# Single 4 KB places for the rows and weights of the first stage, and a first half of x loaded ahead from two queues

## The chip, the cores and the metric

The kernel runs on one core of a Trainium2 chip. The metric is the device time of one execution in microseconds (us). Comparisons use runs of both kernels on the same chip.

## What is computed

One residual block over 1024 tokens of width 1024: three token mixers (a gated linear recurrence, a forgetting attention, and a cross-attention into 256 memory tokens) with sigmoid merge gates, an output projection, and a convolutional gated feed-forward. The first stage of the kernel holds the beginning of it:

```python
h = _rmsnorm(x, norm_mix_g[l])
z = h @ w_in[l]
(hq, hf, hi, hg, fq, fk, fv, ff, mq, gate_logits) = split(z, pts)
...
mem_kv = _rmsnorm(mem, norm_mem_g[l]) @ mem_kv_w[l]
y_c = _memory_mixer(mq, mem_kv, mem_q_norm_g[l], mem_k_norm_g[l])
gates = sigmoid(gate_logits).reshape(B, T, N_BRANCH, D_MODEL)
merged = (gates[:, :, 0] * (y_a @ w_br_hgrn[l]) + gates[:, :, 1] * (y_b @ w_br_fox[l])
          + gates[:, :, 2] * (y_c @ w_br_mem[l]))
x = x + merged @ w_out[l]
x = x + _conv_glu_ffn(_rmsnorm(x, norm_ffn_g[l]), ...)
```

The row norm of x is a factor per token. The kernel multiplies by the gain of the norm first, runs the matmuls on x times gain, and applies the factor (`rt`, spread to `rx`) to the result.

## The kernel before

Every operand of a matmul is split into a high part (`wh`, `uh`), cast on ACT, and a low part (`wl`, `ul`), subtracted on DVE; `mm3` makes three matmuls of each product: high by high, high by low, low by high. A product of 128 x 128 weights with 512 columns is one such group of three.

The first stage is a list of steps, `SEQ`, which the kernel issues one after the other. A scheduler of the framework then places the instructions of each engine by its own estimate of when they can run; each engine takes its instructions in the order so built. The steps that matter here:

- `w0` to `w4` (`first_weights`) split the weights of the first two gate chunks, which lie in `wg[0]` and `wg[1]`. `x0` to `x7` (`x_chunk`) make `uh` and `ul` from the row blocks `xk` of x. `s0` to `s7` (`gate_step`) run the 12 matmuls of one k for two gate chunks and two column halves, 96 in all, into PSUM tiles `lg`, `tr` and `po`.
- `u0` to `u7` (`mem_chunk`) split the memory tokens `mt`; `mn` squares the rows of the memory for their norm.
- `k0` to `k7` (`kv_chunk`) split one quarter of the memory's key or value weights each (`wkv`, 128 x 1024) and run 12 matmuls; k0 to k3 give the keys, k4 to k7 the values. `me` (`keys_out`) normalizes the keys, `mv` writes the values out, `mk` transposes the keys.
- `xn` (`x_norm`) squares the eight row tiles of x, `x_row`, on ACT and DVE in turns, and makes `rt`.
- `f1`, `f2`, `f3` (`differences`) make the operand families T1, T2, T3 of the later dense units from `xk`; T1 and T2 reuse the memory of the row tiles.
- `c0` (`first_cover`) runs the third gate chunk, "the cover": 48 matmuls with the weights `cover_raw`, among which `spread_dma` (PE transpose, ACT copy, two DMAs) spreads `rt` to `rx`. `ev` evaluates the two first gate chunks with `rx`.

Ten matmuls on a constant tile (`NDULL`, line 263), the fillers, run on PE ahead of everything.

`wg`, the memory rows, `wkv` and `x_row` pass through four tiles of two rows each (8 KB of a partition): `T2h` and `T2l` hold `wg` and `wkv`, `T1h` and `T1l` the memory rows and the rows of x. All loads of the stage are issued by the sync engine SP in the order written:

```python
SP.dma_start(cv, vec)
for k in range(KC):
    if k in (0, 2):
        SP.dma_start(wg[k // 2], w_first[k // 2])
    SP.dma_start(xk[k], xT[:, k, :])
```

then the memory, its rows, four `wkv`, the constants, four rows of x, and from there one `wkv` and one row of x in turns. The first cover weights come last in the text. SP takes its queue in order too: a load whose place is still in use holds back those behind it.

After the stage come a fourth gate chunk, the dense units, the attention stages, and the feed-forward, which the change does not touch except for names of tiles.

Of the kernel before, what the change touches and what calls it, by code (L numbers as in the profile page):

```python
# [8 lines left out]
F32 = mybir.dt.float32  # L9
F32R = mybir.dt.float32r  # L10
# [4 lines left out]
P = 128  # L15
T = 1024
# [10 lines left out]

ORDER = [(br, j) for br in (1, 0, 2) for j in range(8)]
NCOVER, NPAIR = 2, 10
NDULL = 10  # L30
NFOX = [0, 3, 0, 3, 0, 3, 1]

_dense = [12, 13, 14, 15] + [16 + 8 * br + j for br, j in ORDER[4:4 + NPAIR]]
# [5 lines left out]
FOX_STEPS, HGRN_STEPS, MEM_STEPS = 28, 14, 7  # L39
AHEAD = 300  # L40
FOX_LATE = 0.2
SEQ = ("w0 x0 s0 w1 x1 s1 w2 x2 s2 w3 x3 s3 w4 x4 s4 x5 s5 x6 s6 x7 s7 u0 u1 u2 u3 mn u4 u5 u6 u7 k0 k1 k2 k3 me k4 k5 k6 k7 mv xn f1 c0 f2 ev mk f3").split()
WFIRST = {0: (0, 1), 1: (1, 2), 2: (2, 3), 3: (3, 4), 4: (4, 8)}
TMIN = -(1.0 - 2.0 ** -24)

# [63 lines left out]
def tile_block(ctx: ExitStack, tc: tile.TileContext, xT, memT, x_rows, mem_rows, vec, fbias, mats, hmask, w_first, w_cm, w_hi, w_fqk, w_fv,  # L109
# [63 lines left out]
    def rstd_small(out, ss, n):  # L173
        w = ss.shape[1]
        V.tensor_scalar(out, ss, 1.0 / n, EPS, ALU.mult, ALU.add)
        return G.tensor_tensor(out, out, mhalf[:, :w], ALU.pow)
# [60 lines left out]
    p0 = Rounded(tc, name="p0", bufs=1, side="right", reuse_waits="tile")  # L237
    fam = {}

    def new_family(pool, name):  # L240
        fam[name] = [pool.tile([P, 4, HB], F32R, tag=f"{name}{p}", name=f"{name}{p}") for p in "hl"]

    pairs = {}

    def row_tile(name):
        t, i, p = pairs.get(name, (None, 2, "l" if name == "T1" else "h"))
        if i == 2:
            p = "hl"[p == "h"] if t is not None else p
            t, i = pt.tile([P, 2, T], F32, tag=name + p, name=f"row{name}"), 0
        pairs[name] = (t, i + 1, p)  # L250
        return t[:, i, :]

    for name in ("T1h", "T1l", "T2h", "T2l"):
        pt.tile([P, 2, T], F32, tag=name, name=f"place{name}")
    umh, uml = (pt.tile([P, KC, NM], F32R, tag=f"T3{p}", name=f"um{p}") for p in "hl")
    mkf = p0.tile([P, 4, NM], F32, tag="mkf", name="mkf")
    mt = p0.tile([P, KC, NM], F32, tag="mt", name="mt")

# [3 lines left out]
    for _ in range(NDULL):  # L262
        PE.matmul(ps_tr()[:, :P], mhalf[:, 0:1].to_broadcast([P, P]), dull, start=True, stop=True)

    wg = [row_tile("T2") for i in range(2)]

    def load_wkv(q):
        wkv.append(row_tile("T2"))
        late["wkv"] = SP.dma_start(wkv[q], w_mkv[q])

    def load_row(i):
        nonlocal last_row
        x_row.append(row_tile("T1"))
        last_row = SP.dma_start(x_row[i], x_rows[i])

    wkv, mem_row, x_row, last_row = [], [], [], None
    SP.dma_start(cv, vec)
    for k in range(KC):
        if k in (0, 2):
            SP.dma_start(wg[k // 2], w_first[k // 2])  # L280
        SP.dma_start(xk[k], xT[:, k, :])
    SP.dma_start(mt, memT)
    for i in range(2):
        mem_row.append(row_tile("T1"))
        SP.dma_start(mem_row[i], mem_rows[i])
    for q in range(4):
        load_wkv(q)
    SP.dma_start(ones, mats[:, P:P + 1])
    SP.dma_start(ident, mats[:, 0:P])
    for i in range(4):  # L290
        load_row(i)
    for i in range(4):
        load_wkv(4 + i)
        load_row(4 + i)
    br, j = order[2]
    cover_raw = raw_weights(w_cm[16 + 8 * br + j], KC * P)
    warm = cp.tile([P, 1], F32, tag="warm", name="warm")
    S.activation(warm, mhalf[:, 0:1], AF.Exp)

# [125 lines left out]
    def gate_step(k):  # L425
        h, l = gw[k // 4]
        for n in range(2):
            for i in range(2):
                sl = slice(n * HB, (n + 1) * HB)
                ws = slice((k % 4) * 256 + i * P, (k % 4) * 256 + (i + 1) * P)  # L430
                mm3(gps[i][n], h[:, ws], l[:, ws], uh[k][:, sl], ul[k][:, sl], k == 0, k == KC - 1)

    def x_norm():
        for i in range(8):
            if i % 2:
                V.tensor_tensor_reduce(out=x_row[i], in0=x_row[i], in1=x_row[i], op0=ALU.mult, op1=ALU.add, scale=1.0,
                                       scalar=0.0, accum_out=rt[:, i:i + 1])
            else:
                late["square"] = S.activation(x_row[i], x_row[i], AF.Square, accum_out=rt[:, i:i + 1])
        rstd_small(rt, rt, D)  # L440

    ybd = tc.dram_tile([P, 4, T], F32, name="ybd")

# [24 lines left out]
    cover = gates_early(NCOVER - 1)  # L468

    def first_cover():  # L470
        wh, wl = weights(None, (KC, P), cover_raw)
        spread = ps_proj()
        pss = [ps_proj(), ps_proj()]
        for n, ps in enumerate(pss):
            sl = slice(n * HB, (n + 1) * HB)
            for k in range(KC):
                late["cover"] = mm3(ps, wh[:, k, :], wl[:, k, :], uh[k][:, sl], ul[k][:, sl], k == 0, k == KC - 1)
                if (n, k) == (0, 2):
                    with tc.issue_after(late["cover"].ins):
                        spread_dma(rx, rt, p0.tile([P, P], F32, tag="line", name="line")[:8, :], "rx", spread)  # L480
        for n, ps in enumerate(pss):
            SP.dma_start(gd[2, n], gate(n, ps))
# [3 lines left out]
            for i in range(2):  # L486
                SP.dma_start(gd[i, n], gate(n, gps[i][n]))

    steps = dict(k=kv_chunk, x=x_chunk, w=first_weights, s=gate_step, u=mem_chunk)
    def family_block(name, k, src, sub=None):  # L490
        h, l = fam[name]
        return split(S, h[:, k, :], l[:, k, :], src, sub)

    def differences():

        b = [[xk[k + 4 * c][:, n * HB:(n + 1) * HB] for c in range(2) for n in range(2)] for k in range(4)]
        new_family(pt, "T1")
        for t in range(4, 8):
            with tc.issue_after(late["keys"].ins):
                S.activation(xk[t], xk[t], AF.Copy, scale=col(C_GX + t))  # L500
        for k, (b11, b12, b21, b22) in enumerate(b):
            with tc.issue_after(late["x_low"].ins):
                V.tensor_sub(b11, b11, b12)
            h, l = (t[:, k, :] for t in fam["T1"])
            S.activation(h, b11, AF.Copy, scale=col(C_GX + k))
            V.scalar_tensor_tensor(out=l, in0=b11, scalar=col(C_GX + k), in1=h.bitcast(F32), op0=ALU.mult, op1=ALU.subtract)
        yield
        new_family(pt, "T2")
        for k, (t1, b12, b21, b22) in enumerate(b):
            V.scalar_tensor_tensor(out=t1, in0=t1, scalar=ngx[:, k:k + 1], in1=b22, op0=ALU.mult, op1=ALU.subtract)  # L510
            family_block("T2", k, t1)
        yield
        new_family(pt, "T3")
        for k, (t2, b12, b21, b22) in enumerate(b):
            V.scalar_tensor_tensor(out=b12, in0=b12, scalar=ngx[:, k:k + 1], in1=b22, op0=ALU.mult, op1=ALU.add)
            family_block("T3", k, b12)
        yield
        yield
        for k, (t2, b12, b21, b22) in enumerate(b):
            V.scalar_tensor_tensor(out=t4[k], in0=t2, scalar=-1.0, in1=b21, op0=ALU.mult, op1=ALU.subtract)  # L520
        pxk.release()
        home["raw"] = Rounded(tc, name="ps2", bufs=1, side="left", reuse_waits="tile")
        new_family(home["raw"], "T4")
        for k in range(4):
            family_block("T4", k, t4[k])
        yield
# [5 lines left out]
            gen["differences"] = differences()  # L532
        next(gen["differences"])

    named = dict(f1=families_step, f2=families_step, f3=families_step, mn=mem_norm, me=keys_out, mk=mem_keys, mv=mem_values, xn=x_norm, ev=first_gates, c0=first_cover)
    for what in SEQ:
        if what in named:
            named[what]()
# [4 lines left out]
    ps1 = Rounded(tc, name="ps1", bufs=1, side="right", reuse_waits="tile")  # L543
    def block(b, k):
        if b in fam:
            return [t[:, k, :] for t in fam[b]]
        c, n = int(b[1]) - 1, int(b[2]) - 1
        return [t[k + 4 * c][:, n * HB:(n + 1) * HB] for t in (uh, ul)]

# [126 lines left out]

    def token_major(src, ncol, evac):

        with tc.issue_after(last_row.ins):
            w = [weights(src[q], (4, ncol)) for q in range(2)]  # L680
        for tb in range(8):
            ps = ps_proj()[:, :ncol]
            tsl = slice(tb * P, (tb + 1) * P)
            for k in range(KC):
                wh, wl = w[k // 4]
                mm3(ps, uh[k][:, tsl], ul[k][:, tsl], wh[:, k % 4, :], wl[:, k % 4, :], k == 0, k == KC - 1)
            evac(tb, ps)
            yield
# [1094 lines left out]
```

## Time and profile before

| | us |
|---|---|
| median of 3 runs | 1708.01 (1707.03 to 1708.39) |
| the profiled execution | 1707.74 |
| its span | 1705.8 |
| PE busy | 1694.4 |
| DVE busy | 1149.1 |
| ACT busy | 801.2 |
| first gate matmul starts | 7.26 |
| memory keys and values on PE | 30.69 to 57.55 |

Times in the profile are counted from the start of the span. A row of the timeline has the start in us, the length in us, the engine, the line of the kernel, the operation, its output and inputs, and a count where equal instructions follow each other; brackets give the idle time before it and what ended it. A row of the list of waits has the waiting engine and line, the releasing one, the total in us, the count, and the longest. A row of the list of DMA issues has the target and source, the queue, the count, the size, and the median time from issue to landing.

### The profile page before, as it was taken

To read this page: it belongs to the slowest core of one execution; us is meant where nothing else is said; L and a number is where in the kernel's file an instruction comes from. 1 tells how busy PE (TensorE), PEld (TensorE's weight loads), DVE (VectorE), ACT (ScalarE), POOL (GpSimd) and SP (SyncE) were. 2 spreads that over 40 slices of the span, in tenths; PEclk is the share of its full clock that TensorE was granted. 3 is DMA by queue.
4 is the path that set the end of the run, shared out by engine and by line. 5 is a ranking of instruction groups with operands and counts; after the bars stand their busy time and mean duration, and the time that the engine had idled before them with its cause. 6 is when DMAs were issued, how large, how long until landed. Compare 5 with 4: busy or idle time off the path is not lost.

```text
span 1705.8 us, 24277 instructions
## 1 busy us (share of the span) xinstructions
PE 1694.4 (99%) x8961; PEld 1454.8 (85%) x8961; DVE 1149.1 (67%) x2057; ACT 801.2 (47%) x1428; POOL 325.7 (19%) x420
## 2 busy tenths in 40 slices
PE   9999999999999999999999999999999999999999
PEld 7788899989898998888888888888888888888887
DVE  6855545665756655786856855897787887765654
ACT  6734446555554554676631334644344444433432
POOL 0100022443432431554310000211111111100000
PEclk9999999999999999999999999999999999999999
DMA  9433142221213111200336552565555445594782
GB/s 381 159 119 123 68 143 87 78 79 57 93 43 99 50 58 57 67 26 19 99 113 227 156 196 99 159 171 160 154 152 142 118 137 152 171 350 156 243 278 87
DMA packets 82486, 227.16 MB, mean 133 GB/s; under 512 B 9648, under 2 KB 12088, under 8 KB 82240
## 3 DMA queue, kind: packets, MB, share of 16 engines
q1 hardware_dynamic: 64320, 161.12, 27.3%
q0 software_dynamic: 18048, 64.50, 13.3%
q8 instruction: 70, 1.15, 0.3%
q14 instruction: 48, 0.39, 0.1%
HBM read 180.72 MB, written 67.93 MB: 146 GB/s over the span
## 4 chain that ended last, share of the span: by engine, by line
PE 95%; DMA 1%; issue 1%; DVE 1%; ACT 0%; POOL 0%; SPq 0%; POOLq 0%; DVEq 0%; ACTq 0%
PE pp L157 21%; PE pp L159 21%; PE pp L158 21%; PE lg L157 4%; PE lg L159 4%; PE lg L158 4%; PE tr L159 2%; PE tr L158 2%; PE tr L157 2%; PE po L934 1%; PE lg L893 1%; PE lg L892 1%; PE po L933 1%; DMA xk<-in_xT 1%; PE tr L921 1%
## 5 line engine op out<-in xcount | busy, mean ns | idle before, releaser
L157 PE MATMUL pp<-uh,wh 128*128 128x512 f32 x412 | 163.2, 396 | 0.0
L158 PE MATMUL pp<-ul,wh 128*128 128x512 f32 x412 | 163.0, 396 | 0.0
L159 PE MATMUL pp<-uh,wl 128*128 128x512 f32 x412 | 162.6, 395 | 0.0
L158 PE MATMUL pp<-wl,uh 128*128 128x256 f32 (+1 forms) x512 | 146.3, 286 | 0.0
L159 PE MATMUL pp<-wh,ul 128*128 128x256 f32 (+1 forms) x512 | 146.0, 286 | 0.0
L157 PE MATMUL pp<-wh,uh 128*128 128x256 f32 (+1 forms) x512 | 145.6, 286 | 0.0
L163 ACT CAST wh<-s 128x512 fp32r<-128x512 f32 x113 | 68.5, 620 | 146.7 <-PE pp L158 75.6
L163 ACT CAST wh<-raw 128x1024 fp32r<-128x1024 f32 (+2 forms) x76 | 67.6, 890 | 103.7 <-PE pp L158 81.8
L163 ACT CAST wh<-rw 128x512 fp32r<-128x512 f32 x87 | 53.3, 620 | 99.3 <-PE pp L158 58.0
L157 PEld LDWEIGHTS pp<-wh,uh 128*128 128x128 f32 x512 | 97.3, 191 | 1.3
L158 PEld LDWEIGHTS pp<-wl,uh 128*128 128x128 f32 x512 | 97.5, 191 | 0.9
L159 PEld LDWEIGHTS pp<-wh,ul 128*128 128x128 f32 x512 | 97.5, 190 | 0.9
L1426 POOL DMA_DIRECT2D rw<-in_w_up x44 | 24.1, 554 | 379.1 <-ACT sqs L1361 163.0
L163 ACT CAST dwh<-wr 128x1024 fp32r<-128x1024 f32 (+1 forms) x41 | 40.2, 980 | 117.7 <-PE tr L158 39.7
L171 DVE TENSOR_TENSOR wl<-raw,wh 128x1024 fp32r<-128x1024 f32 (+2 forms) x75 | 78.0, 1040 | 18.4 <-ACT wh L163 18.3
L159 PEld LDWEIGHTS pp<-uh,wl 128*128 128x128 f32 x412 | 77.5, 188 | 15.0
L157 PEld LDWEIGHTS pp<-uh,wh 128*128 128x128 f32 x412 | 77.5, 188 | 14.6
L158 PEld LDWEIGHTS pp<-ul,wh 128*128 128x128 f32 x412 | 77.6, 188 | 14.5
L908 ACT ACTIVATE pt<-pt,st 128x128 f32<-128x128 f32 (+3 forms) x64 | 49.7, 777 | 40.6 <-DVE st L905 33.5
L171 DVE TENSOR_TENSOR dwl<-wr,dwh 128x1024 fp32r<-128x1024 f32 (+1 forms) x41 | 46.3, 1129 | 32.1 <-ACT dwh L163 32.1
L910 POOL TENSOR_SCALAR pt<-pt,st 128x128 f32<-128x128 f32 (+3 forms) x64 | 50.5, 789 | 77.9 <-DVE st L909 61.7
L898 DVE CUSTOM_DVE_ANT_0 pt<-lg,nf 128x512 f32<-128x512 f32 (+2 forms) x80 | 41.6, 527 | 28.4 <-PE lg L893 14.1
(495 smaller groups left out, 5134.0 us busy)
## 6 DMA issues: line engine op xcount, KB each, us to landing
rw<-in_w_up POOLq DMA_DIRECT2D x44, 512.0 KB, 4.7
sd<-in_w_dn POOLq DMA_DIRECT2D x30, 512.0 KB, 5.9
br<-yd SPq DMA_DIRECT2D x30, 512.0 KB, 5.8
raw<-in_w_cm SPq DMA_DIRECT2D x24, 512.0 KB, 3.5
gd<-gt SPq DMA_DIRECT2D x48, 256.0 KB, 2.0
gt<-gd SPq DMA_DIRECT2D x48, 256.0 KB, 2.7
yd<-fc SPq DMA_DIRECT2D x44, 256.0 KB, 2.4
wr<-sd SPq DMA_DIRECT2D x20, 512.0 KB, 4.7
```

Of the source, the lines that this page charges most:

```text
L157: PE.matmul(ps, lh, rh, start=first, stop=False, skip_group_check=more)
L158: PE.matmul(ps, lh, rl, start=False, stop=False, skip_group_check=more)
L159: return PE.matmul(ps, ll, rh, start=False, stop=last, skip_group_check=more)
L163: return S.copy(out, in_)
L171: return (sub or V).tensor_sub(l, src, h.bitcast(F32))
L892: PE.matmul(ps[:, :w], qa[i][:, tsl], kh[i][:, s0:s0 + w], start=True, stop=False)
L893: fox_sets[p][3] = PE.matmul(ps[:, :w], qa[i][:, tsl], kl[i][:, s0:s0 + w], start=False, stop=True)
L898: V.tensor_tensor_reduce(out=pt[:, s0 + lo:s0 + hi], in0=ps[:, lo:hi], in1=bias, op0=ALU.add, op1=ALU.max, scale=1.0, scalar=-3e38, accum_ ...
L908: S.activation(pt[:, :ns], pt[:, :ns], AF.Exp, bias=st[:, 2:3], accum_out=st[:, 3:4])
L910: G.tensor_scalar(pt[:, :ns], pt[:, :ns], st[:, 3:4], 0.0, ALU.mult, ALU.add)
L921: PE.transpose(ptr[:, jj * 256:jj * 256 + P], pts[0][:, ssl], ident)
L1426: late["raw"] = G.dma_start(raw[:, 2 * i:2 * i + 2, :], src[:, 2 * i:2 * i + 2, :])
```

## The change

The four two-row tiles become eight single rows of 4 KB. The memory rows take two places of T1; the first four `wkv` take the other two of T2 and of T1; the last four `wkv` follow in the first places of T2 and T1 (`lk`, `load_late`); then come four rows of x in the places of the first `wkv` (`lx`) and four in those of T2 (`ly`). The squares of the rows of x become steps of their own (`q0` to `q7`) among `k4` to `k7`, and the cover's weights are loaded by a step, `cw`. T1 and T2 become families of two tiles per part instead of one. At the front, ACT's queue issues the first quarter of the first weight slice, SP loads the first block of x in two halves ahead of the rest of the slice, and the second slice moves from before x's third block to before its fourth. There are 12 fillers instead of 10. The waits by which the early cover weights and the `fv` weights follow the loads refer to the last load of the stage.

```diff
-NDULL = 10
+NDULL = 12
...
-SEQ = ("w0 x0 s0 w1 x1 s1 w2 x2 s2 w3 x3 s3 w4 x4 s4 x5 s5 x6 s6 x7 s7 u0 u1 u2 u3 mn u4 u5 u6 u7 k0 k1 k2 k3 me k4 k5 k6 k7 mv xn f1 c0 f2 ev mk f3").split()
+SEQ = ("w0 x0 s0 w1 x1 s1 w2 x2 s2 w3 x3 s3 w4 x4 s4 x5 s5 x6 s6 x7 s7 u0 u1 u2 u3 mn u4 u5 u6 u7 lk k0 k1 k2 k3 lx "
+       "q0 me k4 q1 k5 ly cw q2 q3 k6 q4 q5 k7 q6 q7 mv xn f1 c0 f2 ev mk f3").split()
...
-    def new_family(pool, name):
-        fam[name] = [pool.tile([P, 4, HB], F32R, tag=f"{name}{p}", name=f"{name}{p}") for p in "hl"]
...
+    def new_family(pool, name, tiles=1):
+        nk = 4 // tiles
+        fam[name] = []
+        for p in "hl":
+            ts = [pool.tile([P, nk, HB], F32R, tag=f"{name}{p}{i}", name=f"{name}{p}{i}") for i in range(tiles)]
+            fam[name].append([ts[k // nk][:, k % nk, :] for k in range(4)])
+
+    def row_tile(place, name):
+        return pt.tile([P, T], F32, tag=place, name=name)
+
+    T1 = [f"T1{p}{i}" for p in "hl" for i in range(2)]
+    T2 = [f"T2{p}{i}" for p in "hl" for i in range(2)]
...
+    def load(place, name, src, eng=SP):
+        t = row_tile(place, name)
+        late["load"] = eng.dma_start(t, src)
+        return t
+
+    wg = [row_tile(T2[i], f"wg{i}") for i in range(2)]
     SP.dma_start(cv, vec)
-    for k in range(KC):
-        if k in (0, 2):
-            SP.dma_start(wg[k // 2], w_first[k // 2])
+    S.dma_start(wg[0][:, :256], w_first[0][:, :256])
+    for i in range(2):
+        SP.dma_start(xk[0][:, i * HB:(i + 1) * HB], xT[:, 0, i * HB:(i + 1) * HB])
+    SP.dma_start(wg[0][:, 256:], w_first[0][:, 256:])
+    for k in range(1, KC):
+        if k == 3:
+            SP.dma_start(wg[1], w_first[1])
         SP.dma_start(xk[k], xT[:, k, :])
     SP.dma_start(mt, memT)
-    for i in range(2):
-        mem_row.append(row_tile("T1"))
-        SP.dma_start(mem_row[i], mem_rows[i])
-    for q in range(4):
-        load_wkv(q)
+    mem_row = [load(T1[i], f"memrow{i}", mem_rows[i]) for i in range(2)]
+    wkv = [load((*T2[2:], *T1[2:])[q], f"wkv{q}", w_mkv[q]) for q in range(4)]
     SP.dma_start(ones, mats[:, P:P + 1])
     SP.dma_start(ident, mats[:, 0:P])
-    for i in range(4):
-        load_row(i)
-    for i in range(4):
-        load_wkv(4 + i)
-        load_row(4 + i)
-    br, j = order[2]
-    cover_raw = raw_weights(w_cm[16 + 8 * br + j], KC * P)
+    x_row = []
+
+    def load_late():
+        wkv.extend(load((*T2[:2], *T1[:2])[q], f"wkv{4 + q}", w_mkv[4 + q]) for q in range(4))
+        late["wkv"] = late["load"]
+
+    def load_rows(first):
+        for i, place in enumerate((*T2[2:], *T1[2:]) if first else T2):
+            x_row.append(load(place, f"xrow{first}{i}", x_rows[len(x_row)]))
...
+    def x_square(i):
+        if i % 2:
+            V.tensor_tensor_reduce(out=x_row[i], in0=x_row[i], in1=x_row[i], op0=ALU.mult, op1=ALU.add, scale=1.0,
+                                   scalar=0.0, accum_out=rt[:, i:i + 1])
+        else:
+            S.activation(x_row[i], x_row[i], AF.Square, accum_out=rt[:, i:i + 1])
+
     def x_norm():
-        for i in range(8):
...
         rstd_small(rt, rt, D)
+
+    def cover_weights():
+        br, j = order[2]
+        late["cover_raw"] = raw_weights(w_cm[16 + 8 * br + j], KC * P)
...
-        new_family(pt, "T1")
+        new_family(pt, "T1", 2)
...
-        new_family(pt, "T2")
+        new_family(pt, "T2", 2)
...
-    with tc.issue_after(late["wkv"].ins):
+    with tc.issue_after(late["load"].ins):
         next(cover)
...
-        with tc.issue_after(last_row.ins):
+        with tc.issue_after(late["load"].ins):
             w = [weights(src[q], (4, ncol)) for q in range(2)]
```

More of the change, by code (lines that the diff above doesn't have):

```diff
@@ L238, in tile_block @@
     fam = {}
-    def new_family(pool, name):
-        fam[name] = [pool.tile([P, 4, HB], F32R, tag=f"{name}{p}", name=f"{name}{p}") for p in "hl"]
[L243 to L255, printed above, removed]
+    def new_family(pool, name, tiles=1):
[8 more added lines that the diff above has]
+    T2 = [f"T2{p}{i}" for p in "hl" for i in range(2)]
+    for place in T1 + T2:
+        row_tile(place, f"place{place}")
+    umh, uml = (pt.tile([P, KC, NM], F32R, tag=f"T3{p}0", name=f"um{p}") for p in "hl")
     mkf = p0.tile([P, 4, NM], F32, tag="mkf", name="mkf")
@@ L263, in tile_block @@
         PE.matmul(ps_tr()[:, :P], mhalf[:, 0:1].to_broadcast([P, P]), dull, start=True, stop=True)
[L265 to L276, printed above, removed]
-    SP.dma_start(cv, vec)
-    for k in range(KC):
-        if k in (0, 2):
-            SP.dma_start(wg[k // 2], w_first[k // 2])
+    def load(place, name, src, eng=SP):
[3 more added lines that the diff above has]
+    wg = [row_tile(T2[i], f"wg{i}") for i in range(2)]
+    SP.dma_start(cv, vec)
+    S.dma_start(wg[0][:, :256], w_first[0][:, :256])
[5 more added lines that the diff above has]
+            SP.dma_start(wg[1], w_first[1])
         SP.dma_start(xk[k], xT[:, k, :])
     SP.dma_start(mt, memT)
-    for i in range(2):
-        mem_row.append(row_tile("T1"))
-        SP.dma_start(mem_row[i], mem_rows[i])
-    for q in range(4):
-        load_wkv(q)
+    mem_row = [load(T1[i], f"memrow{i}", mem_rows[i]) for i in range(2)]
+    wkv = [load((*T2[2:], *T1[2:])[q], f"wkv{q}", w_mkv[q]) for q in range(4)]
     SP.dma_start(ones, mats[:, P:P + 1])
     SP.dma_start(ident, mats[:, 0:P])
-    for i in range(4):
-        load_row(i)
-    for i in range(4):
-        load_wkv(4 + i)
-        load_row(4 + i)
-    br, j = order[2]
-    cover_raw = raw_weights(w_cm[16 + 8 * br + j], KC * P)
+    x_row = []
[5 more added lines that the diff above has]
+            x_row.append(load(place, f"xrow{first}{i}", x_rows[len(x_row)]))
     warm = cp.tile([P, 1], F32, tag="warm", name="warm")
@@ L431, in gate_step @@
                 mm3(gps[i][n], h[:, ws], l[:, ws], uh[k][:, sl], ul[k][:, sl], k == 0, k == KC - 1)
-    def x_norm():
-        for i in range(8):
[L435 to L439, printed above, removed]
+    def x_square(i):
[4 more added lines that the diff above has]
+            S.activation(x_row[i], x_row[i], AF.Square, accum_out=rt[:, i:i + 1])
+    def x_norm():
         rstd_small(rt, rt, D)
+    def cover_weights():
+        br, j = order[2]
+        late["cover_raw"] = raw_weights(w_cm[16 + 8 * br + j], KC * P)
     ybd = tc.dram_tile([P, 4, T], F32, name="ybd")
@@ L470, in first_cover @@
     def first_cover():
-        wh, wl = weights(None, (KC, P), cover_raw)
+        wh, wl = weights(None, (KC, P), late["cover_raw"])
         spread = ps_proj()
@@ L487, in first_gates @@
                 SP.dma_start(gd[i, n], gate(n, gps[i][n]))
-    steps = dict(k=kv_chunk, x=x_chunk, w=first_weights, s=gate_step, u=mem_chunk)
+    steps = dict(k=kv_chunk, x=x_chunk, w=first_weights, s=gate_step, u=mem_chunk, q=x_square)
     def family_block(name, k, src, sub=None):
         h, l = fam[name]
-        return split(S, h[:, k, :], l[:, k, :], src, sub)
+        return split(S, h[k], l[k], src, sub)
     def differences():
         b = [[xk[k + 4 * c][:, n * HB:(n + 1) * HB] for c in range(2) for n in range(2)] for k in range(4)]
-        new_family(pt, "T1")
+        new_family(pt, "T1", 2)
         for t in range(4, 8):
@@ L503, in differences @@
                 V.tensor_sub(b11, b11, b12)
-            h, l = (t[:, k, :] for t in fam["T1"])
+            h, l = (t[k] for t in fam["T1"])
             S.activation(h, b11, AF.Copy, scale=col(C_GX + k))
@@ L533, in families_step @@
         next(gen["differences"])
-    named = dict(f1=families_step, f2=families_step, f3=families_step, mn=mem_norm, me=keys_out, mk=mem_keys, mv=mem_values, xn=x_norm, ev=first_gates, c0=first_cover)
+    named = dict(f1=families_step, f2=families_step, f3=families_step, mn=mem_norm, me=keys_out, mk=mem_keys, mv=mem_values, xn=x_norm, lk=load_late, lx=lambda: load_rows(True), ly=lambda: load_rows(False), cw=cover_weights, ev=first_gates, c0=first_cover)
     for what in SEQ:
@@ L545, in block @@
         if b in fam:
-            return [t[:, k, :] for t in fam[b]]
+            return [t[k] for t in fam[b]]
         c, n = int(b[1]) - 1, int(b[2]) - 1
```

## The prediction

> **What bounds the kernel now.** I read the page first, then the list of waits on PE, then PE's timeline over the first 60 us, which is the whole reach of the change, and last the ACT, DVE and DMA rows beside it.
>
> ```profile
> span 1705.8 us, 24277 instructions
> PE 1694.4 (99%) x8961; PEld 1454.8 (85%) x8961; DVE 1149.1 (67%) x2057; ACT 801.2 (47%) x1428; POOL 325.7 (19%) x420
> PE pp L157 <- ACT wh L163: 1.6, 1, 1.6
> PE lg L157 <- ACT uh L345: 1.6, 1, 1.6
> PE pp L158 <- DVE wl L171: 1.3, 1, 1.3
> ```
>
> PE sets the end, and it is idle for only 1705.8 - 1694.4 = 11.4 us. The three longest waits (waiter, releaser, total, count, longest) all lie in the first stage: one before the first gate matmul, two in the memory keys and values. An edit to this stage can win these waits and the slow clock around them, and not much more.
>
> ```profile
> 1.03 4.63 PE L263 MATMUL tr<-dull,mhalf 128*128 128x128 f32 x20 [1.03 <-POOL dull L261]
> 7.26 0.79 PE L157 MATMUL lg<-uh,wh 128*128 128x512 f32 x1 [1.59 <-ACT uh L345]
> 7.85 0.63 PE L157 MATMUL tr<-uh,wh 128*128 128x512 f32 x1
> 8.28 0.63 PE L157 MATMUL lg<-uh,wh 128*128 128x512 f32 x1
> 10.41 0.44 PE L159 MATMUL tr<-uh,wl 128*128 128x512 f32 x1
> 30.23 0.39 PE L158 MATMUL po<-ul,wh 128*128 128x512 f32 x1
> 30.46 0.39 PE L159 MATMUL po<-uh,wl 128*128 128x512 f32 x1
> 30.69 0.62 PE L157 MATMUL pp<-wh,umh 128*128 128x512 f32 x2
> 46.78 0.39 PE L159 MATMUL tr<-wh,uml 128*128 128x512 f32 x1
> 48.79 0.50 PE L157 MATMUL pp<-wh,umh 128*128 128x512 f32 x1 [1.62 <-ACT wh L163]
> 50.80 0.50 PE L158 MATMUL pp<-wl,umh 128*128 128x512 f32 x1 [1.28 <-DVE wl L171]
> 51.38 0.54 PE L158 MATMUL tr<-wl,umh 128*128 128x512 f32 x1
> 54.70 0.49 PE L157 MATMUL pp<-wh,umh 128*128 128x512 f32 x1
> 57.55 0.39 PE L157 MATMUL pp<-uh,wh 128*128 128x512 f32 x1
> ```
>
> Start, length, instruction. Matmuls step by 8.28 - 7.85 = 0.43 us at first and by 30.46 - 30.23 = 0.23 us (0.227 over many) later: PE has a slow and a fast pace. It is slow until 10.41 and again from 51.38 to 54.70, after the two waits. So before has three blocks: fillers (10 matmuls in 20 passes, 4.63 us, 0.46 us each), gates (96 matmuls, 7.26 to 30.69), and eight wkv chunks (96 matmuls, 30.69 to 57.55). At full pace 96 matmuls take 21.8 us, so the chunks lose 26.86 - 21.8 = 5.1 us: 2.9 of idle and 2.2 of slow pace and restarts. From 57.55, the cover matmuls, PE runs on. The sum below is made for these blocks; what is later is shifted with them, since PE hardly waits there.
>
> **Front: the first matmul.** What is needed shrinks from cv, a 512 KB weight slice and a whole 512 KB row block of x to cv, a 128 KB slice and a 256 KB half.
>
> ```profile
> GB/s 0 0 0 75 184 246 360 352 352 377 352 270 320 393 401 393 369 393 401 451 377 393 410 418 442 426 401 410 418 442 426 434 451 475 393 426 393 377 442 418
> 4.95 1.32 ACT L163 CAST wh<-rowT 128x256 fp32r<-128x256 f32 x4 [1.26 <-DMA rowT<-in_w_first]
> 6.49 1.34 ACT L345 ACTIVATE uh<-xk,cv 128x512 fp32r<-128x512 f32 x2 [0.22 <-DMA xk<-in_xT]
> ```
>
> The first row is the traffic of the first 20 us in 40 slices of 0.5 us. Summed, 1.11 MB (cv, slice, xk0) have moved by about 5.4 us, and ACT gets xk0 at 6.49, some 1.0 later. The changed order needs 0.06 + 0.13 + 0.26 = 0.46 MB: moved by 3.6, usable at about 4.4. Then one half of uh (1.34 / 2 = 0.67) and a hand-over of 0.1: first real matmul at 5.2 instead of 7.26. I take 4.6 (no lag after the bytes) to 6.5 (the smaller pieces land no better than before) as ends.
>
> But four of the twelve fillers are now placed by the build among the gate matmuls of k=0 (eight ahead, then 2, 1 and 1), and PE takes its queue in order. At the slow pace these four cost 4 x 0.46 = 1.85 us after the first real matmul, which is most of the 2.1 won. The rest depends on when the pace turns fast. Before, 4.63 us of fillers did not turn it, with 1.6 us idle behind them; the turns at 10.41, 51.38 and 54.70 lie 12 and 1 times 3.41 us apart, so I place possible turns on such a grid, 7.0 being the one before 10.41.
> - Turn at 10.41 again: 5.2 us of slow pace hold 4 fillers and 7.8 gate matmuls; 88.2 x 0.227 = 20.0; gates end at 30.4, 0.3 earlier.
> - Turn at 7.0: two fillers and 2 matmuls before it, then 2 half-cost fillers (0.46) and 94 x 0.227 = 21.3; end at 28.8, 1.9 earlier.
> I take the middle, -1.1. x arrives early enough for both: xk1 closes the same 1.6 MB in both orders, wg1 only moves from before xk2 to before xk3 and is first used at k=4.
>
> [...]
>
> **Middle: the wkv chunks.** All eight wkv loads now stand ahead of the rows of x in SP's queue, and in ACT's queue no difference step stands before the last two casts. So the casts for wkv6 and wkv7 come in time, and both waits above go. What is late next is the cover: its weights' cast and subtraction stand, in the order that the build gives, behind the steps that were moved.
>
> ```profile
> 23.65 1.05 ACT L338 ACTIVATE rowT<-rowT 128x1024 f32<-128x1024 f32 x1
> 24.69 1.99 ACT L163 CAST wh<-rowT 128x1024 fp32r<-128x1024 f32 x2
> 41.15 0.69 ACT L395 ACTIVATE mkt<-pp,rm 128x512 f32<-128x512 f32 x1 [3.76 <-PE pp L159]
> 41.73 1.04 ACT L163 CAST wh<-rowT 128x1024 fp32r<-128x1024 f32 x1
> 42.80 1.22 DVE L171 TENSOR_TENSOR wl<-rowT,wh 128x1024 fp32r<-128x1024 f32 x1 [4.16 <-ACT wh L163]
> 43.95 0.68 DVE L397 TENSOR_REDUCE mkr<-mkt 128x4 f32<-128x512 f32 x1
> 44.54 1.21 DVE L436 CUSTOM_DVE_ANT_0 rowT<-rowT 128x1024 f32<-128x1024 f32 x1
> 45.68 0.68 DVE L397 TENSOR_REDUCE mkr<-mkt 128x4 f32<-128x512 f32 x1
> 48.32 1.29 DVE L400 TENSOR_TENSOR mkt<-mkt,mkr 128x512 f32<-128x512 f32 x2 [1.75 <-POOL mkr L176]
> 53.61 2.07 DVE L515 SCALAR_TENSOR_TENSOR xk<-xk,ngx,xk 128x512 f32<-128x512 f32 x3
> 55.60 1.22 DVE L171 TENSOR_TENSOR wl<-raw,wh 128x1024 fp32r<-128x1024 f32 x1
> ```
>
> The chain, counted from the start of the first chunk (30.69 before):
> - PE finishes the keys' first half at 41.15 - 30.69 = 10.46. ACT then has mkt 0.58, a row square 1.04, mkt 0.58 and the cast of wkv6 1.04: 13.7.
> - DVE from there without a break: wl of wkv6 1.15, two reductions 1.18, a square 1.14, wl of wkv7 1.15, one tiny step 0.1, two T3 differences 1.33, a square 1.14, a difference 0.66, two mkt products 1.21, a difference 0.66, a square 1.14, two T1 low parts 1.33, and the cover's wl 1.22. Sum 13.4, so 27.1.
> - PE is through its chunks and the cover's first two matmuls at 21.8 + 0.45 = 22.25, and its third needs this wl. It idles 4.9 us, in two parts, since the cover's wh also comes only at 23.3 (ACT: 13.7, then two squares of mkt 1.1, cast of wkv7 1.0, four scalings of xk and a row square 5.2, two T1 casts 1.2, the cast 1.04).
> An idle of 4.9 us makes PE slow again. With the 2.2 us of slow pace and restarts that 2.9 us of idle cost before, the middle loses 7.1 against 5.1: +2.0. Ends: 1.6 us of slow pace (eight matmuls at 0.2 more) and 3.2 (two grid steps), that is +1.4 to +3.4.
>
> **At no cost.** The 4 KB places and the split T1 and T2 families change which buffer waits on which, not the work. SP now holds rows back until the subtraction of the wkv in their place is done; queued behind them are the later rows and the second cover slice (L182), first used after 48 cover matmuls, 11 us behind the cover's start. rt is ready after the last square, through POOL:
>
> ```profile
> 57.88 1.86 POOL L176 TENSOR_TENSOR rt<-rt,mhalf 128x8 f32<-128x8 f32 x1
> ```
>
> On DVE four steps of 0.66 lie between the cover's wl and the step for POOL, so rt comes 2.6 + 0.2 + 1.9 = 4.7 us after the wl, and PE's transpose of it is built behind 22 more cover matmuls, at least 22 x 0.227 = 5.0 us after. If that cover failed, each us would be one us of PE. The first load from ACT's queue delays only the table load, and ACT then waits for data anyway.
>
> **Sum.** The profiled execution took 1707.74 us around its span of 1705.8; the median of three is 1708.01, 0.3 above. 1707.74 - 1.1 + 2.0 = 1708.6. No difference of under 0.2% (3.4 us) can be told from none here. Ends: -1.9 - 1.0 (a turn of the pace even earlier) + 1.4 to +0.3 + 3.4 gives 1706.2 to 1711.4.
>
> **Rivals.**
> 1. The two waits go and nothing takes their place, because the row squares and differences overlap better than in my chain. For it: the waits were for exactly these casts. Against: DVE's 13.4 us are steps in one in-order queue, with known durations. Price -5.1 - 1.1: 1701.5. Chance 0.11.
> 2. Slower, by late rows in front of the cover's wl. The sixth row of x takes wkv5's place, free at about +10.7, and DVE wants it at 13.7 + 6.0 = +19.7: 9 us.
>
> ```profile
> rowT<-in_x_rows SPq DMA_DIRECT2D x8, 512.0 KB, 8.6
> rowT<-in_mem_rows SPq DMA_DIRECT2D x2, 512.0 KB, 11.2
> ```
>
> Landing took 8.6 us in the median and 11.2 for the memory rows, behind a full queue. From 9 us on each us is a us of PE; at 12 it is 3.0: 1711.6. Against: by then most of the queue is drained. Chance 0.16.
> 3. The change does not do what it says at the front: first matmul at 6.5, fillers after it, nothing won: 1707.74 + 2.0 = 1709.7. Chance 0.10.
>
> The forecast keeps 0.63. It and rival 3 are within 0.2%: 0.73, less 0.01 for what reaches beyond; faster 0.11, slower 0.17. The range takes the forecast's own ends and rival 2 up to 1712.0, and leaves rival 1 out: 1705.5 to 1712.0.
>
> **What would show it.** Right: first gate matmul near 5.2, gates' end between 28.5 and 30.7, no PE wait inside the wkv chunks, then two waits at the cover, on ACT wh and on DVE wl, of about 1.5 and 3.4 us, with matmuls of 0.43 us behind. Wrong: no wait at the cover (rival 1), a wait of DVE for in_x_rows ahead of it (rival 2), gates ending later than 30.7, or PE waiting at the rt transposes or for rx.

## The result, and the profile after

Over 22 executions of each, the changed kernel takes 1711.39 us in the median (1707.49 to 1715.14) and the kernel before 1707.24 (1704.82 to 1713.02). The ratio is 1.0020, with a 95% interval of 1.0012 to 1.0028; it is that of the means (1711.08 against 1707.72), and the medians alone give 1.0024. Timed once more beside the experiments (11 against 33 executions) it took 1708.84 against 1707.01: ratio 1.0014, interval 1.0005 to 1.0022. So the change makes the kernel slower by 0.05 to 0.28%, around the bound of 0.2% below which the prediction calls it no difference. The profiled execution took 1708.91 us and is one of the quicker ones of the changed kernel, at a mean granted clock (the share of its full clock that PE was allowed) of 0.999 where others list down to 0.996; it shows only a part of the difference between the medians.

The time goes with that clock. Of the 22 executions, the 7 at 0.999 take 1708.8 us in the mean, the 8 at 0.997 take 1711.9 and the 4 at 0.996 take 1714.0: 1.7 us for each 0.001. At 0.999 the executions of the second comparison agree, with 1708.7 (4 executions), beside 1706.8 for the kernel before (26). So at the same clock the change costs 1.9 us, and the rest of the medians' difference comes with the lower clock.

From the page of the changed kernel, and then from the list of its waits on PE (waiter, releaser, total, count, longest):

```profile
span 1707.1 us, 24290 instructions
PE 1693.6 (99%) x8965; PEld 1453.3 (85%) x8965; DVE 1148.8 (67%) x2057; ACT 801.1 (47%) x1428; POOL 325.5 (19%) x420
```

```profile
PE pp L160 <- DVE wl L172: 3.3, 1, 3.3
PE pp L160 <- DVE fa L1521: 1.4, 1, 1.4
PE pp L158 <- ACT wh L164: 1.2, 1, 1.2
...
PE tr L756 <- ACT msq L753: 1.0, 1, 1.0
PE lg L158 <- ACT uh L343: 0.8, 2, 0.5
```

The wait before the first gate matmul has shrunk to 0.5 us, and those inside the wkv chunks are gone. The first and third waits are the forecast ones at the cover (lines have moved by one to four). The second (`fa`, rows of the feed-forward, at 1090 us) and the fourth (`msq`, squares in the memory mixer, near 232 us) are not in the prediction. The change touches neither place in the code, and before they were shorter:

```profile
PE pp L159 <- DVE fa L1518: 0.8, 1, 0.8
...
PE tr L753 <- ACT msq L750: 0.5, 1, 0.5
```

PE's timeline of the changed kernel (start, length, instruction, idle time before it):

```profile
1.03 3.78 PE L263 MATMUL tr<-dull,mhalf 128*128 128x128 f32 x16 [1.03 <-POOL dull L261]
5.33 0.49 PE L158 MATMUL lg<-uh,wh 128*128 128x512 f32 x1 [0.52 <-ACT uh L343]
...
28.86 0.62 PE L158 MATMUL pp<-wh,umh 128*128 128x512 f32 x2
...
51.98 0.50 PE L158 MATMUL pp<-uh,wh 128*128 128x512 f32 x1 [1.19 <-ACT wh L164]
...
56.02 0.59 PE L160 MATMUL pp<-uh,wl 128*128 128x512 f32 x1 [3.31 <-DVE wl L172]
56.41 0.63 PE L158 MATMUL pp<-uh,wh 128*128 128x512 f32 x1
56.84 0.63 PE L159 MATMUL pp<-ul,wh 128*128 128x512 f32 x1
...
59.40 0.54 PE L159 MATMUL pp<-ul,wh 128*128 128x512 f32 x1
```

The gates end at 28.86, 1.83 earlier than before (30.69), and the chunks run through without a wait. Then PE waits 1.19 and 3.31 us at the cover, and its matmuls step by 0.43 us until 59.4.

Where the rest went is read from the same four instructions in the timelines of both kernels, the kernel before in the first fence and the changed one in the second. The `Vf` row writes values of the attention, the `x1d` row stores a part of x after the mixers, `B11h` is an operand of the feed-forward, and the fourth row is the last matmul.

```profile
218.43 0.48 ACT L708 ACTIVATE Vf<-pp,rt 128x256 f32<-128x256 f32 x1 [0.33 <-PE pp L159]
1069.55 0.32 SPq L1363 DMA_DIRECT2D x1d<-sum  x1
1090.07 0.50 PE L159 MATMUL pp<-B11h,wl 128*128 128x512 f32 x1 [0.80 <-DVE fa L1518]
1701.53 0.39 PE L159 MATMUL po<-dbh,dwl 128*128 128x512 f32 x1
```

```profile
218.11 0.48 ACT L711 ACTIVATE Vf<-pp,rt 128x256 f32<-128x256 f32 x1 [0.33 <-PE pp L160]
1069.72 0.32 SPq L1366 DMA_DIRECT2D x1d<-sum  x1
1091.51 0.50 PE L160 MATMUL pp<-B11h,wl 128*128 128x512 f32 x1 [1.39 <-DVE fa L1521]
1702.98 0.39 PE L160 MATMUL po<-dbh,dwl 128*128 128x512 f32 x1
```

At 218 us the changed kernel is 0.32 us ahead; at 1070 us it is 0.17 behind, lost at the wait for `msq` near 232 us; at 1090 us it is 1.44 behind, and so it stays to the end (1.45). So in the profiled pair the edited stage gives 0.3 us, the wait near 232 us takes 0.5, and a stage that nobody edited takes 1.27.

### The profile page after: what moved, and what is told of

Same layout as the page of the kernel before. It is cut to its first block, busy times and chain, and to the rows that moved or that the text cites. A ratio compares the mean times of both kernels' runs of the same rounds, so it can differ in the third digit from the quotient of the medians.

```text
span 1707.1 us, 24290 instructions
## 1 busy us (share of the span) xinstructions
PE 1693.6 (99%) x8965; PEld 1453.3 (85%) x8965; DVE 1148.8 (67%) x2057; ACT 801.1 (47%) x1428; POOL 325.5 (19%) x420
## 4 chain that ended last, share of the span: by engine, by line
PE 97%; DVE 1%; DMA 1%; ACT 1%; issue 0%; SPq 0%; POOL 0%; POOLq 0%; ACTq 0%
PE pp L158 21%; PE pp L160 21%; PE pp L159 21%; PE lg L158 4%; PE lg L160 4%; PE lg L159 4%; PE tr L158 2%; PE tr L160 2%; PE tr L159 2%; PE po L937 1%; PE lg L896 1%; PE lg L895 1%; PE po L936 1%; PE po L158 1%; PE po L160 1%; PE po L159 1%
## 5 line engine op out<-in xcount | busy, mean ns | idle before, releaser
L159 PEld LDWEIGHTS pp<-ul,wh 128*128 128x128 f32 x412 | 78.0, 189 | 14.7
```

The lines of the kernel that those rows point to most:

```text
L159: PE.matmul(ps, lh, rl, start=False, stop=False, skip_group_check=more)
```

## The experiments

Four theories were told apart. A: the excess is the wait at the cover with the slow matmuls behind it (a stretch at half clock is here called a spell; in the profile after the granted clock is 0.50 for 3.41 us, from 56.28 to 59.69, and that would cost 1.7 if PE were at work throughout). B: it lies late in the kernel. C: the front costs. D, formed after the first four runs: the weight pool's tiles moved to other addresses, and that costs 1.27 us at 1090.

**e1_again** is the changed kernel unedited.

> The changed kernel again, for a second profile and more times. Theory A (the middle's slow-pace term is too small): beyond the profiled run's one slow spell of 3.41 us at the cover, other executions of the kernel have more such spells, each worth 3.41 x (1 - 0.5) = 1.7 us, all between 45 and 70 us of the trace; median near 1711, mean granted clock lower by 0.001 for each spell. Theory B (something late in the kernel): the extra spells or waits lie after 100 us. Theory C (the front): the pace turns fast at 5.0 in one execution and at 8.4 or later in another.

It took 1708.84 us (1707.84 to 1712.67). One row of the table by stretches, the 20 us from 40 us on (busy times of PE, PEld, DVE, ACT and POOL, then the granted clock, the DMA share and GB/s), first of the profile after and then of this one:

```profile
40.00:60.00 20.00, 15.50 (x61) 12.06 (x59) 18.08 (x30) 20.00 (x32) 4.56 (x4) 0.91 0.41 139
```

```profile
40.00:60.00 20.00, 15.50 (x61) 12.03 (x60) 18.08 (x29) 20.00 (x31) 4.23 (x4) 0.84 0.38 134
```

PE's busy time is the same, but the clock falls further: a mean of 0.84 over 20 us means 2 x 0.16 x 20 = 6.4 us at half clock, 0.91 means 3.6. So the same waits bring one spell or two. But most of the second spell lies in the wait, where PE has nothing to do (e1_again):

```profile
54.00:56.00 2.00, 0.00 (x0) 0.00 (x0) 2.00 (x3) 2.00 (x4) 0.00 (x0) 0.50 0.00 0
```

Its matmuls are slow from 56.36 to 59.94, those of the profile after from 56.41 to 59.40. From the start of the chunks to the `Vf` row (29.20 to 218.73, and 28.86 to 218.11) the two take 189.5 and 189.3 us. So the second spell cost about 0.3 us here and not theory A's 1.7: of its half clock only the part that fell on work counted. Theory A does not account for the step at 1090 us, which this profile has too (again a wait of 1.4 us for `fa`): B is right for that part. As for C, the pace at the front differs little between the two:

```profile
5.66 0.60 PE L263 MATMUL tr<-dull,mhalf 128*128 128x128 f32 x4
```

```profile
5.77 0.61 PE L263 MATMUL tr<-dull,mhalf 128*128 128x128 f32 x4
```

Both the profile after (first) and this one run their fillers behind the first gate matmul at the fast pace, 0.15 us a pass.

**e2_front** is the kernel before with the changed front alone.

```diff
-NDULL = 10
+NDULL = 12
+    S.dma_start(wg[0][:, :256], w_first[0][:, :256])
+    for i in range(2):
+        SP.dma_start(xk[0][:, i * HB:(i + 1) * HB], xT[:, 0, i * HB:(i + 1) * HB])
+    SP.dma_start(wg[0][:, 256:], w_first[0][:, 256:])
...
```

> The front alone: order of the first loads, first slice from ACT's queue, halves and 12 fillers as changed; places, later loads and order of steps as before. Theory A: the front gains 1.8 us (gates end at 28.9 and not 30.7), the two waits inside the wkv chunks are back (1.6 and 1.3 us), no wait of over 1 us at the cover; 1705.4, that is 1.8 under the kernel before, ratio 0.9989. Theory C (the front is what costs): gates end later than 30.0 in the profile or the median is 1 to 3 us over the kernel before, ratio 1.001 or more. Theory B: level with the kernel before, 1707.

It took 1707.25 us, ratio 1.0004 (0.9995 to 1.0013): nothing won in the time, and less than theory C's loss. In its profile the front does win: the `Vf` row that lay at 218.43 stands 1.46 earlier. Two rows of its timeline, and then one of its table by stretches:

```profile
216.97 0.48 ACT L712 ACTIVATE Vf<-pp,rt 128x256 f32<-128x256 f32 x1 [0.33 <-PE pp L159]
231.70 1.05 PE L757 MATMUL tr<-ones,msq 128*128 128x1 f32 x8 [0.91 <-ACT msq L754]
```

```profile
220.00:240.00 20.00, 19.09 (x148) 18.88 (x148) 6.79 (x9) 5.99 (x11) 4.21 (x3) 0.91 0.40 135
```

Then PE waits 0.91 us for `msq`, which ACT makes from a transfer (`mqf`), and the granted clock of this stretch is 0.91 where all other profiles have 1.00: a spell. In this profile the gain is lost there. This wait was 0 to 1.0 us in the profiles of this case without an order by kernel (0.5 before, 1.0 after, 0.3 in e1_again, none in e3_back), so it varies from execution to execution, and no run ties it to the change.

**e3_back** is the changed kernel with the front of before.

```diff
-NDULL = 12
+NDULL = 10
+    for k in range(KC):
+        if k in (0, 2):
+            SP.dma_start(wg[k // 2], w_first[k // 2])
...
```

> The rest without the front: first loads and 10 fillers as before, places, later loads and order of steps as changed. Theory A: first real matmul at 7.3, two waits at the cover of 1.3 and 3.3 us, slow spells there; 1.8 us over the changed kernel, so near 1713, 5 to 6 us over the kernel before, ratio 1.0032. Theory C: level with the kernel before, within 1 us, 1707. Theory B: as the changed kernel, 1711.

It took 1709.56 us, ratio 1.0019 (1.0010 to 1.0028): 2.6 over the kernel before, and 0.7 over the changed kernel in the same comparison, not 1.8 as expected. So the back of the change costs about 2.6 (3.2 by the means), and the front gives back less than the profile's 1.83. The profiles show where a part went: at the `Vf` row e3_back is 1.68 behind the profile after (219.79 against 218.11), at the `x1d` row only 0.42 (1070.14 against 1069.72), since it has no wait for `msq`.

**e4_fill** puts matmuls without use into the cover's idle time.

```diff
+        for _ in range(18):
+            with tc.issue_after(late["kv"].ins):
+                PE.matmul(spread[:, :HB], uh[0][:, :P], uh[0][:, :HB], start=True, stop=True)
```

> The changed kernel with 18 matmuls of 128x512 (uh by uh, result unused) between the last wkv chunk and the cover: they fill the idle time of 1.2 + 3.3 us with 18 x 0.227 = 4.1 us of work, so PE should stay at its fast pace. Theory A (slow spells from the cover's wait are the excess): the wait's own 4.5 us stays, as fillers, but the spells go; 1.7 us (one spell) to 5 us (three) under the changed kernel, 1706.5 to 1709.5, and no slow matmuls between 50 and 62 us. Rival (the spells have no part in the excess, the waits or later stages alone do): no gain, or 0.5 us slower because the fillers push the cover back.

```profile
40.00:60.00 20.00, 19.45 (x86) 15.79 (x85) 18.08 (x30) 19.96 (x30) 3.84 (x4) 1.00 0.38 133
```

1707.84 us, ratio 1.0007 (0.9998 to 1.0016), 1.0 under the changed kernel, with the clock at 1.000 in all eleven executions (0.997 to 0.999 there). That is less than the 1.7 expected of even one spell; by the means it is 1.6 (1707.91 against 1709.51), so the two can't be told apart. The profile has two new waits, 0.55 us at the cover's start and 0.62 at 88 us, which take a part. The cover's third matmul comes no earlier after the chunks' start than in the profile after (27.6 us against 27.2), so what went is the slow pace alone: theory A's spells are real, and on balance taking them away is worth 1 to 1.6 us.

**e5_raw_first** and **e6_raw_last** test theory D. The weight pool `wp` hands out addresses in the order in which its tags first come. Before, `cover_raw` was claimed at the start, so `raw` lay at the bottom, below `wh` and `wl`. The change claims it in the step `cw`, after the gate weights; `wh` lies at the bottom now and `raw` on top. Near 1060 us the pool is released, and the next one puts its `rw` tiles over the bottom addresses, in both kernels. POOL loads them once their former users are through. Before, ACT releases the first load at 1059.80; now a matmul on PE, the reader of the tiles that lie there, releases it 14.7 us later. POOL issues these loads (start, length, row, count, what ended the idle time); before first, then the changed kernel, with DVE's wait for the transfer:

```profile
1059.80 1.05 POOL L1426 DMA_DIRECT2D rw<-in_w_up  x2 [163.03 <-ACT sqs L1361]
```

```profile
1074.47 1.06 POOL L1429 DMA_DIRECT2D rw<-in_w_up  x2 [177.54 <-PE lg L160]
1083.34 2.10 DVE L1421 TENSOR_TENSOR s<-rw 128x512 f32<-128x512 f32 x1 [2.44 <-DMA rw<-in_w_up]
```

e5_raw_first is the changed kernel with the old order, e6_raw_last the kernel before with the new one:

```diff
+    for _ in range(2):
+        wp.tile([P, 4 * 264], F32, tag="raw", name="raw", bufs=2)
```

```diff
+    for t in ("wh", "wl"):
+        for _ in range(3):
+            wp.tile([P, 4 * 264], F32R, tag=t, name=t, bufs=3)
```

> The changed kernel with two places of raw claimed when the weight pool is opened, so that raw lies at the bottom of the pool's addresses as before, below wh and wl. Theory D (the moved places cost): in the changed kernel the first rw pieces of the second MLP weights, which lie at the bottom of the same addresses, wait for a matmul on wl and are issued at 1074.5 and not 1059.8; DVE then waits 2.4 us for rw and PE loses 1.3 us near 1087. With raw back, rw is issued near 1060, the PE waits for fa are 0.7 us and not 1.4, the wait for B21l is gone, and the kernel is 1.3 us faster than the changed one: 1707.5 against 1708.8, ratio to before 1.0006. Theory A (all of it is the cover's wait and its slow spells): no difference to the changed kernel, 1708.8, ratio 1.0014.

> The kernel before with its weight pool's places claimed in the changed kernel's order (three wh, three wl, then raw), nothing else changed. Theory D: rw is issued near 1074.5, DVE waits 2.4 us for it, PE's wait for fa is 1.4 us; 1.3 us slower than before, 1708.3, ratio 1.0008, while the first 1000 us are as before. Theory A: no difference, 1707.0.

e5 (first fence) and e6 (second):

```profile
1060.38 1.06 POOL L1431 DMA_DIRECT2D rw<-in_w_up  x2 [163.04 <-ACT sqs L1366]
1070.14 0.32 SPq L1368 DMA_DIRECT2D x1d<-sum  x1
1090.65 0.50 PE L162 MATMUL pp<-B11h,wl 128*128 128x512 f32 x1 [0.79 <-DVE fa L1523]
```

```profile
1068.07 0.32 SPq L1366 DMA_DIRECT2D x1d<-sum  x1
1072.83 1.07 POOL L1429 DMA_DIRECT2D rw<-in_w_up  x2 [177.53 <-PE lg L162]
1081.75 2.04 DVE L1421 TENSOR_TENSOR s<-rw 128x512 f32<-128x512 f32 x1 [2.50 <-DMA rw<-in_w_up]
1089.87 0.50 PE L162 MATMUL pp<-B11h,wl 128*128 128x512 f32 x1 [1.40 <-DVE fa L1521]
```

From the `x1d` row to the PE row it is 20.51 us in e5, as before (1090.07 - 1069.55 = 20.52), and 21.80 in e6, as in the changed kernel (1091.51 - 1069.72 = 21.79). The order of a pool's first claims is worth 1.27 us; nothing else differs in the code of these two from their originals. The other profiles agree: all twelve of this case take 20.51 to 20.53 us here with `raw` at the bottom, and 21.79 or 21.80 with `wh` there. The times agree in sign: e5 1707.93 us, ratio 1.0005 (0.9996 to 1.0014) and e6 1709.24, ratio 1.0014 (1.0005 to 1.0023), beside a kernel before of 1707.35. Only e6's difference is clear of the noise; e5 and the changed kernel stand in different comparisons, and their intervals overlap.

**e7_raw_fill** joins e4 and e5.

> Both mends on the changed kernel: raw at the bottom, and the 18 matmuls between the wkv chunks and the cover. Theories A and D together: the fillers' 1.0 us and the places' 1.3 us add up: 1706.5, ratio 0.9997, clock 1.000 in nearly all executions. If they don't add (the time won is lost at a later wait for a transfer, such as mqf near 232 us): 1707.5 or more.

1706.26 us, ratio 0.9995 (0.9986 to 1.0004). That is the expected sum, and with both mends the change is no longer slower than before.

**e8_squares** takes e5 and moves DVE's and ACT's work: k7 moves ahead of q4 and q5, a step `cs` splits the cover's weights right behind it, the last four squares wait for that split, and the differences for the squares.

```diff
-k6 q4 q5 k7 q6 q7 mv xn f1 c0
+k6 k7 cs q4 q5 q6 q7 mv xn f1 c0
...
+        with tc.issue_after(late["split low" if i % 2 else "split cast"].ins):
+            square(i)
...
+            with tc.issue_after(late["square S"].ins), tc.issue_after(late["square V"].ins):
+                S.activation(h, b11, AF.Copy, scale=col(C_GX + k))
+                V.scalar_tensor_tensor(out=l, in0=b11, scalar=col(C_GX + k), in1=h.bitcast(F32), op0=ALU.mult, op1=ALU.subtract)
```

> The changed kernel with raw at the bottom, the cover's split put right behind the last wkv chunk's split, the row squares behind it and the differences of x behind the squares. By theory A the wait at the cover (1.2 + 3.3 us) and its slow spells go, and with D 1.3 us more: if nothing is given back, 1709.0 - 4.5 - 1.7 - 1.3 = 1701.5. The rival: DVE's queue of the first 100 us is only put in another order, so PE waits for the differences later (two waits of 0.6 and 1.5 us between 70 and 90 us, and a shorter lead at the T4 products): 1705 to 1706.5, ratio 0.999.

The first waits on PE under 120 us, and the last matmul of the timeline:

```profile
PE lg L160 <- ACT uh L346: 1.3, 3, 0.5
PE pp L162 <- DVE wl L174: 1.2, 1, 1.2
...
PE pp L160 <- DVE gt L464: 0.6, 1, 0.6
PE lg L162 <- DVE wl L174: 0.3, 1, 0.3
```

```profile
1698.25 0.39 PE L162 MATMUL po<-dbh,dwl 128*128 128x512 f32 x1
```

1704.23 us, ratio 0.9985 (0.9977 to 0.9994): faster than both kernels, and between the two expectations. The cover's 4.5 us are gone; the waits that come in their place (0.6, 0.3 and 1.2, between 69 and 86 us) sum to 2.1. The rival was right that DVE's queue gives a part back, but its price of 1705 to 1706.5 was a little high. The last matmul comes 4.73 us earlier than in the changed kernel, 1.27 of it by e5's part. Which of the moves did the rest was not taken apart.

**e9_old_front** and **e10_fill8** vary e8's front: the first has the loads and ten fillers of before, the second 8 fillers, none of them among the gate matmuls.

> The version e8_squares with the first loads and the ten fillers of the kernel before. Theory A (the front is worth its 1.8 us where no later wait eats it): first real matmul near 7.2 instead of 5.3, gates end 1.8 us later, and as the waits at 230 us are short there too, the time is 1.5 to 2 us over e8_squares: 1706.0, ratio to before 0.9993. Rival (the front's gain is always lost again, at the wait for mqf near 232 us, as in e2_front): 1704.2 to 1704.8, ratio 0.9985.

> The version e8_squares with 8 fillers and not 12, so that none stands among the gate matmuls of the first block of x. The prediction priced the four at 1.85 us at the slow pace, 0.9 at the fast one. Theory A: PE waits for the next halves of uh there anyway (1.3 us in three waits), so they lie in that wait: within 0.3 us of e8_squares, 1704.2, and waits for uh about 0.9 us longer. Rival 1 (they cost what they last): 0.9 us faster, 1703.3. Rival 2 (without them the pace falls back): a slow spell of 3.4 us before 15 us, 1.7 us slower, 1705.9.

e9 took 1706.44 us, ratio 0.9997 (0.9988 to 1.0006), 2.2 over e8 (timed in another comparison, with the kernel before at 1707.24 and 1707.35). In the profiles the chunks start 1.63 us later (31.02 against 29.39) and the last matmul comes 2.04 later. So here the new front keeps its worth to the end, and the rival falls. e10 took 1705.19, ratio 0.9989 (0.9980 to 0.9998), between e8 and rival 2. Its profile says more than the time. The chunks start at 28.48 and not at e8's 29.39, so without the four fillers the gates do end 0.9 us earlier, which theory A denied; but PE then waits 1.6 us for `wl` on DVE, in two waits, where e8 waits 0.3:

```profile
28.48 0.62 PE L160 MATMUL pp<-wh,umh 128*128 128x512 f32 x2
1698.13 0.39 PE L162 MATMUL po<-dbh,dwl 128*128 128x512 f32 x1
```

```profile
PE lg L162 <- DVE wl L174: 1.6, 2, 1.3
```

The last matmul differs from e8's by 0.12 us. What the front wins here is taken by DVE at 90 us. The median is 1.0 over e8, the mean only 0.3 (1705.15 against 1704.86), and the intervals overlap, so the times show no difference.

## Why the prediction was right in its verdict, and where it was not

- **The front: right mechanism, undersized.** First gate matmul forecast at 5.2, measured 5.33; gates' end 1.83 earlier, at the end of the range (0.3 to 1.9), where the middle, 1.1, was taken. The mis-sized term is the turn of the pace: the middle gave half its weight to a turn at 10.41, and no profile with this front is slow that late. The profile after is fast from its first gate matmul on (5.33); the latest turn is e5_raw_first's, where the four fillers at the same place are still slow and the pace is fast from 7.07:

```profile
5.78 1.06 PE L265 MATMUL tr<-dull,mhalf 128*128 128x128 f32 x4
```

  Yet e5's gates end at 28.91, so the case "turn at 7.0" (28.8) was the better one. Over the seven profiles with this front and twelve fillers the end lies between 28.86 and 29.70; behind the first matmul their waits for `uh`, 0 to 1.1 us, are a term that the sum put at nothing. In time the front gave less: 0.7 between e3 and e1, nothing in e2, 2.2 between e9 and e8. Part of it is lost wherever something later waits.
- **The fillers: right at the fast pace.** Without them the gates end at 28.48 (e10), 0.4 to 1.2 us before those seven. That fits the price at the fast pace, 0.9, and not the 1.85 at the slow one.
- **The middle: right.** The waits measured 1.19 and 3.31 us, forecast 1.5 and 3.4, and about eight matmuls behind them were slow, the lower case of the forecast. DVE's chain ran as summed, from the cast of wkv6 to the cover's low part:

```profile
42.60 1.23 DVE L172 TENSOR_TENSOR wl<-wkv,wh 128x1024 fp32r<-128x1024 f32 x1 [1.92 <-ACT wh L164]
54.75 1.21 DVE L172 TENSOR_TENSOR wl<-raw,wh 128x1024 fp32r<-128x1024 f32 x1
```

  54.75 + 1.21 - 28.86 = 27.1 after the chunks' start, the forecast figure. The middle lost 1.83 - 0.32 = 1.5 us in the profiled pair, at the low end of +1.4 to +3.4. (The upper end was added wrongly: 4.9 + 3.2 - 5.1 is 3.0, and the range's upper end built on it would be 1711.0 and not 1711.4.)
- **The spells: right in the profile, undersized over the executions.** The slow pace was priced as one value for one execution. It is a draw: one spell in the profile after, two in e1_again, none with fillers (e4). e4 shows that this part is worth 1 to 1.6 us in the second comparison. The first comparison's median lies 2.6 us above the second's, and its executions list lower clocks (0.9976 in the mean against 0.9982). Where in the kernel those further spells lie is not shown; no profile here has a clock as low as 0.996.
- **"At no cost": the step that failed.** The prediction let the places change "which buffer waits on which, not the work", and looked at the first stage only. The moved claim of `cover_raw` turned the weight pool's addresses round and cost 1.27 us at 1090 us (e5, e6). The other claim of that part held: PE does not wait at the `rt` transpose (63.16).
- **Sum.** Forecast for the profiled execution: -1.1 + 2.0 = +0.9. Its own: -1.8 + 1.5 + 0.5 (`msq`) + 1.3 (`rw`), less 0.3 behind the last matmul, +1.2 (1708.91 against 1707.74). Four errors of 0.5 to 1.3 us that nearly cancel: the verdict of a small loss was right, the sum by luck closer than its terms. Over the executions the loss is larger than the +0.9: 3.4 us by the means in the first comparison, where the median is 2.8 above the forecast 1708.6, and 2.6 in the second. And a loss of under 0.2% could be told from none: the interval 1.0005 to 1.0022 lies clear of 1.
- **Rivals.** 1 falls: the cover's waits did take the place of the two that went. 2 falls: DVE has no wait for `in_x_rows` between 42.60 and 54.75. 3 falls: the front gained.

With the same front the turn of the pace moves from execution to execution: fast by 5.33 in the profile after, not yet at 5.78 in e5_raw_first. The prediction placed it by the rows of one execution, that of the kernel before.

## What to carry to other kernels

A load that is moved in the text also moves its tile in a pool that hands out addresses by first claim (1.27 us here): ask which later tile lies over those addresses, and what it will wait for. Price a wait on PE with the slow matmuls that may follow, as a draw with several outcomes (one spell in the profile after, two in e1_again), and count only the half clock that falls on work (0.3 us of the second spell there). Read the gain of an early edit at the next place where PE depends on another engine, not at the edit's end. When an engine's queue feeds the next stage in order (DVE here), look at that order as well as at the loads: moving the urgent split ahead took 3.7 us off e5 in the same comparison, where the new front gave 2.2 at most. That order was not tried without the moved loads.

## What the runs showed of the hardware

A wait as short as 0.91 us was followed by slow matmuls, when eight matmuls of a single column came behind it (e2_front at 231.70): the 20 us around have a granted clock of 0.91. The same eight matmuls behind a wait of 0.97 us in the profile after brought none (1.00), so the wait's length alone does not decide. In e9_old_front PE started its gates fast and fell back after two matmuls, behind a wait of 2.00 us:

```profile
7.36 0.50 PE L160 MATMUL lg<-uh,wh 128*128 128x512 f32 x1 [2.00 <-ACT uh L342]
7.70 0.40 PE L160 MATMUL tr<-uh,wh 128*128 128x512 f32 x1
7.98 0.67 PE L160 MATMUL lg<-uh,wh 128*128 128x512 f32 x1
8.44 0.63 PE L160 MATMUL po<-uh,wh 128*128 128x512 f32 x1
```

Starts step by 0.34 and 0.28 us, then by 0.46. The twenty filler passes took 4.33 us here and 4.63 before; with the two short steps that reads as a pace that was fast already and was lost again behind the wait. e6_raw_last, with the same first loads, does the same behind a wait of 1.80 us: its twenty filler passes took 4.10 us, and the starts step by 0.33 and 0.28 us, then by 0.56 and 0.42. That the wait is the cause was not tested. So in three profiles the slow pace stood behind a wait of 0.91, 1.80 and 2.00 us.
